# A decoder block on one core: a third pair of k tiles by seven products in the gate/up blocks, moves issued by Pool, own places for those weights, and PSUM banks that alternate

## The chip, the cores and the metric

The kernel runs on one core of a Trainium2 chip. Its time is the device time of one execution in microseconds (us). The kernel before took 1382.08 us, the median of three runs (1381.11 to 1382.55).

## The reference, cut to what matters

One decoder layer on 256 rows of width 2048: two attention mixers, a gated sum of them, LayerNorm, then a SwiGLU sublayer and a second LayerNorm. The change lies in the first half of the SwiGLU sublayer, whose hidden width is 5632 (11 blocks of 512 columns):

```
def _swiglu(h, w_ffn_in, w_ffn_out):
    g, u = jnp.split(h @ w_ffn_in, 2, axis=-1)
    return (jax.nn.silu(g) * u) @ w_ffn_out

h = _layer_norm(DEEPNORM_ALPHA * h + _swiglu(h, w_ffn_in[l], w_ffn_out[l]), ln2_g[l], ln2_b[l])
```

All is float32.

## The kernel before, in words

**Products.** A float32 product is made of three matmuls in the type fp32r. Each operand is split into a rounded part and the rest: `split` casts on ScalarE (L71) and subtracts on VectorE (L72). `mm3` (L91 to L93) adds high x high, high x low and low x high into one bank. The 256 rows are two row tiles m of 128, the depth of 2048 is sixteen k tiles of 128. The rows stand still in TensorE; weights stream through, 512 columns a matmul.

**The gate/up blocks.** Block j (0 to 10) makes the 512 gate columns and the 512 up columns of its number for both row tiles, so four sums: c11, c12 (gate and up of row tile 0), c21, c22 (row tile 1). Block 0 is made in another way. For j = 1 to 10 `pair_product` goes over eight pairs of k tiles. For each it loads four tiles of 128 x 512 in one DMA of 1 MB (`load_pair`, L697): gate and up columns of the two k tiles. A plain pair has two splits of 1024 columns, g and u, and eight `mm3`, which are 24 matmuls.

**A pair by seven.** The four sums over one pair are a 2 x 2 by 2 x 2 product of blocks, and seven products of sums of blocks can stand in for eight. The pairs named in `SEVEN` do this in blocks 1 to 9. VectorE builds four sums of weight tiles in place in the loaded tile (L737 to L740, a chain in which each step needs the one before), then these are split too (names t2 and t3): 128 x 1024 twice. So such a pair has three splits of 1024, one of 512 (u: only one of the two up tiles is needed as it is) and the chain of four, and seven `mm3`, which are 21 matmuls. The sums of rows that they need are made and split once, in `row_forms`. Four of the seven products don't belong to one sum alone: they gather over all pairs by seven of the block in four banks of their own (`ps_`, products 1, 6, 7 and 5). After the last pair by seven of a block L751 to L755 join these into four tiles p1, u2, u3 and u4, and at the block's end L758 to L761 add them to the banks c11 to c22. A sigmoid (L774) and two multiplications per row tile follow (L775, L787), then a transpose of 32 x 32 blocks into the tile rt (L264), of which there is one (tag tab). Sixteen DMAs (`move_blocks`, L286) carry rt into act, the input of the output product. `later(8, ...)` places them in the program eight ticks on; a plain pair and a pair by seven tick twice each.

**Buffers.** Weights as loaded: three places (tag raw). Split weights: eight for the high part and eight for the low part (tags wh, wl), each 128 x 1024. Scratch of 128 x 512: eight (tag s). PSUM: four banks of tag acc (c11 to c22) and four of tag tmp (the products). Tag big: twelve places of 8 KB a partition, which in the gate/up blocks hold hres (2), hth and htl (the normalised rows, high and low, 4), the row forms (1), and act, one tile for two blocks.

**Order.** The order on each engine in these blocks is set by a planner, not by hand. It takes instructions in the order of the program, and lets later ones go first where an earlier one isn't ready in its own estimate. SP issues all DMAs of these blocks: loads of weights and moves. After block 10 the output product follows (names fo, oacc): 44 k tiles, the first row tile in acc, the second in tmp from the third k tile on; its rows (ahl, tag s) are split from act.

The functions that the diff touches and what calls them:

Of the kernel before, what the change touches and what calls it, by code (L numbers as in the profile page):

```python
# [11 lines left out]
F32 = mybir.dt.float32  # L12
F32R = mybir.dt.float32r
# [4 lines left out]
P = 128  # L18
# [11 lines left out]
N = 512  # L30
# [14 lines left out]
def decoder_block(ctx, tc, xT, x, wz, lam_qk, subln, wa, wb, wo, g1, b1, b1T, wf, wfp, wfo, g2, b2,  # L45
                  cs_a, cs_b, out):
    nc = tc.nc
    const = ctx.enter_context(tc.tile_pool(name="const", bufs=1))
    wp = ctx.enter_context(tc.tile_pool(name="wp", bufs=8))
    big = ctx.enter_context(tc.tile_pool(name="big", bufs=12))  # L50
    sp = ctx.enter_context(tc.tile_pool(name="sp", bufs=8))
# [3 lines left out]
    def bigt(shape, dt, name):  # L55
        return big.tile([P] + shape, dt, tag="big", name=name)

    def scr(name):
        return sp.tile([P, N], F32, tag="s", name=name)
# [4 lines left out]
    def acc(name):  # L64
        return ps.tile([P, N], F32, tag="acc", name=name)

    def tmp(name):
        return ps.tile([P, N], F32, tag="tmp", name=name)

    def split(src, hi, lo, eng=None):  # L70
        nc.scalar.copy(hi, src)  # L71
        (eng or nc.vector).tensor_sub(lo, src, hi)  # L72
# [17 lines left out]
    def mm3(ac, xh, xl, wh, wl, start, stop):  # L90
        nc.tensor.matmul(ac, xh, wh, start=start, stop=False)  # L91
        nc.tensor.matmul(ac, xh, wl, start=False, stop=False)  # L92
        nc.tensor.matmul(ac, xl, wh, start=False, stop=stop)  # L93
# [10 lines left out]
    def tick():  # L104
        clock[0] += 1
        if queue and queue[0][0] <= clock[0]:
            queue.pop(0)[1]()
# [175 lines left out]
    def move_blocks(dst, rt):  # L283
        for i in range(4):
            for b in range(4):
                nc.sync.dma_start(dst[32 * b:32 * b + 32, i], rt[32 * i:32 * i + 32, b])  # L286

    def qk_block(blk, cs, half, qk, w, name):
        first = blk == 0
# [363 lines left out]
    def stat_h(m, kt):  # L653
        return hth[m][:, kt, :], htl[m][:, kt, :]
# [15 lines left out]

    SEVEN = (2, 4)
    forms = []

    def row_forms():
        ns = len(SEVEN)
        full = bigt([NM, 2 * ns, P], F32, "hfull")
        fs = bigt([4, ns, P], F32, "forms")
        hl = bigt([2, 4, ns, P], F32R, "formshl")  # L680
        for m in range(NM):
            for n, i in enumerate(SEVEN):
                nc.vector.tensor_add(full[:, m, 2 * n:2 * n + 2, :], hth[m][:, 2 * i:2 * i + 2, :], htl[m][:, 2 * i:2 * i + 2, :])
        a = [[full[:, m].rearrange("p (n t) q -> p n t q", t=2)[:, :, t, :] for t in range(2)] for m in range(NM)]
        nc.vector.tensor_add(fs[:, 0], a[1][0], a[1][1])
        nc.vector.tensor_sub(fs[:, 1], fs[:, 0], a[0][0])
        nc.vector.tensor_sub(fs[:, 2], a[0][0], a[1][0])
        nc.vector.tensor_sub(fs[:, 3], a[0][1], fs[:, 1])
        split(fs, hl[:, 0], hl[:, 1])
        forms.append(hl)  # L690

    def stat_s(f, n):
        return forms[0][:, 0, f - 1, n, :], forms[0][:, 1, f - 1, n, :]

    def load_pair(j, i):
        raw = wp.tile([P, 4, N], F32, tag="raw", name="raw_fp%d_%d" % (j, i), bufs=3)
        nc.sync.dma_start(raw.rearrange("p a n -> p (a n)"), wfp[j - 1][i])  # L697
        return raw

    def halves(src, name):  # L700
        n = src.shape[1]
        wh = wp.tile([P, 2, N], F32R, tag="wh", name="wh" + name)
        wl = wp.tile([P, 2, N], F32R, tag="wl", name="wl" + name)
        split(src, wh[:, 0:n], wl[:, 0:n])
        return [(wh[:, a, :], wl[:, a, :]) for a in range(n)]


    def pair_product(j):
        nk = KD // 2
        seven = SEVEN if j < NB_F - 1 else ()  # L710
        c11, c12, c21, c22 = [acc("acc_f%s_%d" % (c, j)) for c in ("g0", "u0", "g1", "u1")]
        ps_ = {}
        for i in range(nk):
            nm = "fp%d_%d" % (j, i)
            raw = load_pair(j, i)
            k0, k1 = 2 * i, 2 * i + 1
            first, final = i == 0, i == nk - 1
            if i not in seven:
                b11, b21 = halves(raw[:, 0:2], nm + "g")
                b22, b12 = halves(raw[:, 2:4], nm + "u")  # L720
                for ac, m, w0, w1 in ((c11, 0, b11, b21), (c12, 0, b12, b22), (c21, 1, b11, b21), (c22, 1, b12, b22)):
                    mm3(ac, *stat_h(m, k0), *w0, first, False)
                    mm3(ac, *stat_h(m, k1), *w1, False, final)
                tick()
                tick()
                continue
            n = seven.index(i)
            s0, s1 = n == 0, n == len(seven) - 1
            if s0:
                for f in (1, 6, 7, 5):  # L730
                    ps_[f] = tmp("p%d_%d" % (f, j))
            b11, b21 = halves(raw[:, 0:2], nm + "g")
            b22, = halves(raw[:, 2:3], nm + "u")
            mm3(ps_[1], *stat_h(0, k0), *b11, s0, s1)
            mm3(c11, *stat_h(0, k1), *b21, False, False)
            mm3(c12, *stat_s(4, n), *b22, False, False)
            nc.vector.tensor_sub(raw[:, 2], raw[:, 2], raw[:, 3])  # L737
            nc.vector.tensor_sub(raw[:, 3], raw[:, 3], raw[:, 0])
            nc.vector.tensor_add(raw[:, 0], raw[:, 2], raw[:, 0])
            nc.vector.tensor_sub(raw[:, 1], raw[:, 1], raw[:, 0])  # L740
            t2, t4 = halves(raw[:, 0:2], nm + "t2")
            t3, t1 = halves(raw[:, 2:4], nm + "t3")
            tick()
            mm3(ps_[6], *stat_s(2, n), *t2, s0, s1)
            mm3(ps_[7], *stat_s(3, n), *t3, s0, s1)
            mm3(ps_[5], *stat_s(1, n), *t1, s0, s1)
            mm3(c21, *stat_h(1, k1), *t4, False, False)
            tick()
            if s1:
                p1, u2, u3, t = [scr("%s_%d" % (c, j)) for c in ("p1", "u2", "u3", "u4")]  # L750
                nc.scalar.copy(p1, ps_[1])  # L751
                nc.vector.tensor_add(u3, p1, ps_[6])
                nc.vector.tensor_add(u2, u3, ps_[7])
                nc.vector.tensor_add(u3, u3, ps_[5])
                nc.vector.tensor_add(t, u2, ps_[5])  # L755
        if not seven:
            return (c11, c12), (c21, c22)
        nc.vector.tensor_add(p1, p1, c11)  # L758
        nc.vector.tensor_add(u3, u3, c12)
        nc.vector.tensor_add(u2, u2, c21)  # L760
        nc.vector.tensor_add(t, t, c22)  # L761
        return (p1, u3), (u2, t)

    act = []
    for j in range(NB_F):
        if j % 2 == 0:

            act.append(bigt([2, 4, NM, 4, 32], F32, "act%d" % (j // 2)))
        rt = None
        ts_ = []  # L770

        def silu(m, gate):
            t = scr("sl%d_%d" % (j, m))
            nc.scalar.activation(t, gate, AF.Sigmoid)  # L774
            nc.vector.tensor_mul(t, t, gate)  # L775
            return t
        if j == 0:
            ts_ = [silu(m, ga[m]) for m in range(NM)]
            later(3, row_forms)
            ups = product(wf[1], KD, stat_h, "fu0")  # L780
        else:
            rows = pair_product(j)
            ts_ = [silu(m, rows[m][0]) for m in range(NM)]
            ups = [rows[m][1] for m in range(NM)]
        rt = sp.tile([P, 4, NM, P], F32, tag="tab", name="rt%d" % j, bufs=1)
        for m in range(NM):
            nc.vector.tensor_mul(ts_[m], ts_[m], ups[m])  # L787
            turn_blocks(rt, m, ts_[m])
        later(8, lambda j=j, rt=rt: move_blocks(act[j // 2][:, j % 2].rearrange("p i m h c -> p i (m h c)"),
                                                rt.rearrange("p b m n -> p b (m n)")))  # L790
# [97 lines left out]
    with tc.manual_schedule():  # L888
# [26 lines left out]
        j = NB_D - 1  # L915
# [74 lines left out]
```

## Time and profile before

| | us |
|---|---|
| median of three runs | 1382.08 |
| profiled execution | 1384.11 |
| its span, first to last instruction | 1382.3 |
| TensorE busy (PE) | 1365.0 |
| VectorE busy (DVE) | 916.9 |
| ScalarE busy (ACT) | 644.5 |
| GpSimd busy (POOL) | 57.2 |

The mean granted clock of TensorE is 0.998. The gate/up blocks 1 to 10 lie between 705 and 1132 us of the span. Times in rows count from the span's start. A matmul's row shows 0.39 us, but the next may start before it has ended; so what counts is the distance from start to start. The same holds on VectorE for instructions that don't wait for each other.

### The profile page before, as it was taken

Reading aid. Unit: us, or ns where it says so; the run is one execution under the profiler, and the core shown is the slowest. Engines: PE = TensorE matmul, PEld = TensorE weight load, DVE = VectorE, ACT = ScalarE, POOL = GpSimd, SP = SyncE. Lnnn points to the kernel's source line nnn. Section 1 sums busy time; section 2 is a strip of 40 time slices with the busy share of each in tenths; the row PEclk is TensorE's granted clock in tenths of the full one; section 3 lists DMA queues with packets and bytes.
Section 4 is the critical chain, followed back from the end, with each engine's and each line's share of the span. In section 5 each row is a group of like instructions: output and inputs, shape, how many; then the busy total and the mean of one; then the engine's idle time right before and its main releaser. Section 6 shows DMA issues by size and latency. Waiting matters only on the chain.

```text
span 1382.3 us, 16276 instructions
## 1 busy us (share of the span) xinstructions
PE 1365.0 (99%) x6110; PEld 1126.0 (81%) x6110; DVE 916.9 (66%) x1161; ACT 644.5 (47%) x866; POOL 57.2 (4%) x64
## 2 busy tenths in 40 slices
PE   8999999999999999999999999999999999999997
PEld 6888888888888888888888888888788788888886
DVE  6666566766645454575878888888787765554555
ACT  4463444546444434443644455445454444444441
POOL 0001010100000000100000000000000000000003
PEclk9999999999999999999999999999999999999999
DMA  8583645464454649663445664546745676555541
GB/s 281 192 302 145 223 166 198 179 217 152 156 225 162 249 138 356 221 244 122 161 161 192 248 244 182 195 171 247 254 170 195 230 280 225 206 186 191 205 152 61
DMA packets 57151, 279.45 MB, mean 202 GB/s; under 512 B 10224, under 2 KB 22640, under 8 KB 25712
## 3 DMA queue, kind: packets, MB, share of 16 engines
q1 hardware_dynamic: 56784, 278.08, 55.2%
q8 instruction: 48, 0.79, 0.2%
q10 hardware_dynamic: 288, 0.33, 0.1%
q14 instruction: 31, 0.25, 0.1%
HBM read 264.74 MB, written 2.10 MB: 193 GB/s over the span
## 4 chain that ended last, share of the span: by engine, by line
PE 79%; DVE 9%; DMA 7%; ACT 2%; issue 2%; SPq 1%; POOL 0%; POOLq 0%; ACTq 0%; DVEq 0%
PE oacc L91 6%; PE oacc L93 6%; PE oacc L92 6%; DMA raw_fp<-in_wfp 5%; PE acc_fu L91 3%; PE acc_fu L93 3%; PE acc_fu L92 3%; PE acc_fg L91 3%; PE acc_fg L93 3%; PE acc_fg L92 3%; PE acc_gA L91 2%; PE acc_gB L93 2%; PE acc_gA L93 2%; PE acc_gA L92 2%; PE acc_gB L92 2%; PE acc_gB L91 2%
## 5 line engine op out<-in xcount | busy, mean ns | idle before, releaser
L72 DVE TENSOR_TENSOR wl_fo<-raw_fo,wh_fo 128x1024 fp32r<-128x1024 f32 x84 | 102.5, 1225 | 98.5 <-ACT wh_fo L71 93.4
L71 ACT CAST wh_fo<-raw_fo 128x1024 fp32r<-128x1024 f32 x84 | 88.2, 1055 | 115.4 <-PE oacc L93 99.2
L93 PE MATMUL oacc<-wh_fo,ahl 128*128 128x512 f32 x332 | 129.3, 389 | 0.0
L91 PE MATMUL oacc<-wh_fo,ahl 128*128 128x512 f32 x332 | 129.2, 389 | 0.0
L92 PE MATMUL oacc<-wl_fo,ahl 128*128 128x512 f32 x332 | 129.2, 389 | 0.0
L93 PEld LDWEIGHTS oacc<-wh_fo,ahl 128*128 128x128 f32 x332 | 62.3, 188 | 13.4 <-DVE ahl L72 0.3
L91 PEld LDWEIGHTS oacc<-wh_fo,ahl 128*128 128x128 f32 x332 | 62.3, 188 | 12.9
L92 PEld LDWEIGHTS oacc<-wl_fo,ahl 128*128 128x128 f32 x332 | 62.3, 188 | 12.9
L72 DVE TENSOR_TENSOR wl_gA<-raw_gA,wh_gA 128x1024 fp32r<-128x1024 f32 x32 | 38.9, 1220 | 35.9 <-ACT wh_gA L71 35.7
L72 DVE TENSOR_TENSOR wl_o<-raw_o,wh_o 128x1024 fp32r<-128x1024 f32 x32 | 39.5, 1235 | 33.9 <-ACT wh_o L71 33.9
L71 ACT CAST wh_gA<-raw_gA 128x1024 fp32r<-128x1024 f32 x32 | 33.6, 1054 | 53.3 <-PE acc_brB L93 20.0
L71 ACT CAST wh_o<-raw_o 128x1024 fp32r<-128x1024 f32 x32 | 33.7, 1054 | 48.5 <-PE acc_o L93 33.9
L72 DVE TENSOR_TENSOR wl_gB<-raw_gB,wh_gB 128x1024 fp32r<-128x1024 f32 x32 | 38.6, 1222 | 19.9 <-ACT wh_gB L71 19.3
L91 PE MATMUL acc_o<-wh_o,mth 128*128 128x512 f32 x128 | 50.4, 394 | 0.0
L91 PE MATMUL acc_gA<-wh_gA,xth 128*128 128x512 f32 x128 | 50.2, 392 | 0.0
L91 PE MATMUL acc_gB<-wh_gB,xth 128*128 128x512 f32 x128 | 50.1, 391 | 0.0
L93 PE MATMUL acc_o<-wh_o,mtl 128*128 128x512 f32 x128 | 49.9, 390 | 0.0
L92 PE MATMUL acc_o<-wl_o,mth 128*128 128x512 f32 x128 | 49.8, 389 | 0.0
L93 PE MATMUL acc_gB<-wh_gB,xtl 128*128 128x512 f32 x128 | 49.8, 389 | 0.0
L92 PE MATMUL acc_gA<-wl_gA,xth 128*128 128x512 f32 x128 | 49.8, 389 | 0.0
L92 PE MATMUL acc_gB<-wl_gB,xth 128*128 128x512 f32 x128 | 49.8, 389 | 0.0
L93 PE MATMUL acc_gA<-wh_gA,xtl 128*128 128x512 f32 x128 | 49.8, 389 | 0.0
(515 smaller groups left out, 3761.9 us busy)
## 6 DMA issues: line engine op xcount, KB each, us to landing
raw_fp<-in_wfp SPq DMA_DIRECT2D x80, 1024.0 KB, 5.9
raw_fo<-in_wfo SPq DMA_DIRECT2D x44, 1024.0 KB, 4.8
raw_gA<-in_wz SPq DMA_DIRECT2D x16, 1024.0 KB, 4.9
raw_gB<-in_wz SPq DMA_DIRECT2D x16, 1024.0 KB, 5.0
raw_o<-in_wo SPq DMA_DIRECT2D x16, 1024.0 KB, 4.8
raw_vA<-in_wz SPq DMA_DIRECT2D x8, 1024.0 KB, 5.1
raw_qB<-in_wz SPq DMA_DIRECT2D x8, 1024.0 KB, 6.9
raw_kB<-in_wz SPq DMA_DIRECT2D x8, 1024.0 KB, 5.2
```

What stands on the lines that cost most here:

```text
L71: nc.scalar.copy(hi, src)
L72: (eng or nc.vector).tensor_sub(lo, src, hi)
L91: nc.tensor.matmul(ac, xh, wh, start=start, stop=False)
L92: nc.tensor.matmul(ac, xh, wl, start=False, stop=False)
L93: nc.tensor.matmul(ac, xl, wh, start=False, stop=stop)
```

## The change

`SEVEN` names three pairs, 2, 4 and 6 (the third, fifth and seventh). The row forms have a third set, in two tiles of tag s. The moves of a block go out from GpSimd's queue. In blocks 1 to 7 the loaded weights of a pair by seven have a place of tag big instead of one of the three of tag raw. In odd blocks the sums lie in the banks of tag acc and the products in those of tag tmp, in even blocks the other way round.

```
     def move_blocks(dst, rt):
         for i in range(4):
             for b in range(4):
-                nc.sync.dma_start(dst[32 * b:32 * b + 32, i], rt[32 * i:32 * i + 32, b])
+                nc.gpsimd.dma_start(dst[32 * b:32 * b + 32, i], rt[32 * i:32 * i + 32, b])
...
-    SEVEN = (2, 4)
+    SEVEN = (2, 4, 6)
...
-        hl = bigt([2, 4, ns, P], F32R, "formshl")
+        hl = bigt([2, 4, 2, P], F32R, "formshl")
+        more = [[sp.tile([P, 4, P], F32R, tag="s", name="forms%d_%d" % (n, k)) for k in range(2)] for n in range(2, ns)]
...
-        split(fs, hl[:, 0], hl[:, 1])
-        forms.append(hl)
+        split(fs[:, :, 0:2], hl[:, 0], hl[:, 1])
+        for n in range(2):
+            forms.append([hl[:, k, :, n] for k in range(2)])
+        for n, hi_lo in enumerate(more):
+            split(fs[:, :, 2 + n], *hi_lo)
+            forms.append(hi_lo)
...
     def load_pair(j, i):
-        raw = wp.tile([P, 4, N], F32, tag="raw", name="raw_fp%d_%d" % (j, i), bufs=3)
+
+        if i in SEVEN and j < 8:
+            raw = bigt([4, N], F32, "raw_fp%d_%d" % (j, i))
+        else:
+            raw = wp.tile([P, 4, N], F32, tag="raw", name="raw_fp%d_%d" % (j, i), bufs=3)
...
-        c11, c12, c21, c22 = [acc("acc_f%s_%d" % (c, j)) for c in ("g0", "u0", "g1", "u1")]
+
+        acc_c, acc_p = (acc, tmp) if j % 2 else (tmp, acc)
+        c11, c12, c21, c22 = [acc_c("acc_f%s_%d" % (c, j)) for c in ("g0", "u0", "g1", "u1")]
...
-                    ps_[f] = tmp("p%d_%d" % (f, j))
+                    ps_[f] = acc_p("p%d_%d" % (f, j))
```

## Rows read from the trace of the kernel before

**Rows 1.** The page, parts 1 and 2: busy time of engines; TensorE's granted clock.

```profile
PE 1365.0 (99%) x6110; PEld 1126.0 (81%) x6110; DVE 916.9 (66%) x1161; ACT 644.5 (47%) x866; POOL 57.2 (4%) x64
...
PEclk9999999999999999999999999999999999999999
```

**Rows 2.** Timeline of TensorE, block 1: start, duration, line, output and inputs.

```profile
710.70 0.39 PE L91 MATMUL acc_fg<-whfp_1g,hth 128*128 128x512 f32 x1
...
715.91 0.39 PE L93 MATMUL acc_fu<-whfp_1u,htl 128*128 128x512 f32 x1
716.14 0.39 PE L91 MATMUL p<-whfp_2g,hth 128*128 128x512 f32 x1
...
720.90 0.39 PE L91 MATMUL acc_fg<-whfp_3g,hth 128*128 128x512 f32 x1
```

**Rows 3.** Busy time by stretch: PE, PEld, DVE, ACT, POOL; block 3.

```profile
789.00:831.00 42.00, 42.00 (x187) 34.79 (x186) 35.83 (x43) 20.91 (x23) 0.00 (x0) 1.00 0.58 212
```

**Rows 4.** Timeline of VectorE, block 7, pairs 3 and 4; in brackets: idle before.

```profile
968.26 1.22 DVE L72 TENSOR_TENSOR wlfp_3g<-raw_fp,whfp_3g 128x1024 fp32r<-128x1024 f32 x1
...
970.53 1.22 DVE L72 TENSOR_TENSOR wlfp_4g<-raw_fp,whfp_4g 128x1024 fp32r<-128x1024 f32 x1
...
972.39 0.69 DVE L737 TENSOR_TENSOR raw_fp<-raw_fp 128x512 f32<-128x512 f32 x1
...
974.57 0.69 DVE L740 TENSOR_TENSOR raw_fp<-raw_fp 128x512 f32<-128x512 f32 x1
976.46 2.36 DVE L72 TENSOR_TENSOR wlfp_4t<-raw_fp,whfp_4t 128x1024 fp32r<-128x1024 f32 x2 [1.20 <-ACT whfp_4t L71]
```

**Rows 5.** Timeline of VectorE, the end of block 7.

```profile
985.69 0.68 DVE L752 TENSOR_TENSOR u<-p,p 128x512 f32<-128x512 f32 x1
986.47 0.69 DVE L753 TENSOR_TENSOR u<-u,p 128x512 f32<-128x512 f32 x1
...
1001.07 0.68 DVE L758 TENSOR_TENSOR p<-p,acc_fg 128x512 f32<-128x512 f32 x1
1001.66 0.68 DVE L737 TENSOR_TENSOR raw_fp<-raw_fp 128x512 f32<-128x512 f32 x1
...
1006.47 0.70 DVE L264 STREAM_TRANSPOSE rt<-sl 128x512 f32<-128x512 f32 x1
1007.10 0.65 DVE L787 TENSOR_TENSOR sl<-sl,u 128x512 f32<-128x512 f32 x1
```

**Rows 6.** Timeline of ScalarE, the end of block 10 and the output product's start.

```profile
1126.98 1.06 ACT L71 CAST wh_fo<-raw_fo 128x1024 fp32r<-128x1024 f32 x1 [0.31 <-PE acc_fu L93]
...
1131.06 0.60 ACT L774 ACTIVATE sl<-acc_fg 128x512 f32<-128x512 f32 x1 [2.12 <-PE acc_fg L93]
1131.55 1.01 ACT L71 CAST ahl<-act 128x256 fp32r<-128x256 f32 x3
```

**Rows 7.** Views of the tiles act and ln2g: issues, ns, first and last start.

```profile
L286 SPq DMA_DIRECT2D act<-rt x176: 507/589/1592, 709.7 to 1144.2; - x176
...
L795 SPq DMA_DIRECT2D ln2g<-in_g x1: 382/382/382, 1074.2 to 1074.2; - x1
```

**Rows 8.** Timeline of VectorE and TensorE, block 1, pair 4.

```profile
722.04 2.36 DVE L72 TENSOR_TENSOR wlfp_4t<-raw_fp,whfp_4t 128x1024 fp32r<-128x1024 f32 x2 [1.20 <-ACT whfp_4t L71]
...
729.06 0.39 PE L91 MATMUL p<-whfp_4t,formshl 128*128 128x512 f32 x1
```

**Rows 9.** Waits of TensorE, whole span: total, times, longest.

```profile
PE acc_fg L91 <- DVE p L758: 2.4, 3, 1.4
```

**Rows 10.** Waits of SP's queue, 747 to 1088 us.

```profile
SPq L286 <- DVE rt L264: 89.1, 8, 11.9
```

**Rows 11.** Timeline of SP's queue, block 4.

```profile
836.37 10.95 SPq L286 DMA_DIRECT2D act<-rt  x16
847.42 16.30 SPq L697 DMA_DIRECT2D raw_fp<-in_wfp  x6
```

**Rows 12.** View of the tile raw_fp: its loads.

```profile
DMA to landing us min/median/max: 4.7/5.9/7.7
```

More of the change, by code (lines that the diff above doesn't have):

```diff
@@ L688, in row_forms @@
         nc.vector.tensor_sub(fs[:, 3], a[0][1], fs[:, 1])
-        split(fs, hl[:, 0], hl[:, 1])
-        forms.append(hl)
+        split(fs[:, :, 0:2], hl[:, 0], hl[:, 1])
[4 more added lines that the diff above has]
+            forms.append(hi_lo)
     def stat_s(f, n):
-        return forms[0][:, 0, f - 1, n, :], forms[0][:, 1, f - 1, n, :]
+        return tuple(t[:, f - 1, :] for t in forms[n])
     def load_pair(j, i):
-        raw = wp.tile([P, 4, N], F32, tag="raw", name="raw_fp%d_%d" % (j, i), bufs=3)
+        if i in SEVEN and j < 8:
+            raw = bigt([4, N], F32, "raw_fp%d_%d" % (j, i))
+        else:
+            raw = wp.tile([P, 4, N], F32, tag="raw", name="raw_fp%d_%d" % (j, i), bufs=3)
         nc.sync.dma_start(raw.rearrange("p a n -> p (a n)"), wfp[j - 1][i])
```

## The prediction

> **What bounds the kernel now.** I read the page first: TensorE is busy 1365.0 of 1382.3 us at the full granted clock, VectorE 916.9 [rows 1]. So a matmul less is time less, as long as nobody else becomes late. I then read the gate/up blocks, the only stretch that the diff touches, from the timeline of TensorE: a pair of k tiles done plainly takes 5.44 us (710.70 to 716.14), one done by seven products 4.76 us (716.14 to 720.90) [rows 2]. A block j = 1 to 9 is now six plain pairs and two by seven: 6 x 5.44 + 2 x 4.76 = 42.16 us, and TensorE fills it. The table by block shows the engine behind it: in a 42 us stretch VectorE is busy 35.83 us where all its records are there (43), and ScalarE 20.91 [rows 3]. VectorE is thus the engine to watch, and its timeline prices a pair. A plain pair is two splits, 968.26 to 970.53: 2.27 us. A pair by seven starts at 970.53 and its last split starts 1.14 after 976.46 and leaves VectorE 1.14 later, at 978.74: 8.21 us, of which 1.20 is idle, waiting for ScalarE's cast of what VectorE itself has just written [rows 4]. The end of a block is fourteen more instructions (L752 to L755, L758 to L761, two each of L775, L787 and the transpose), 0.59 to 0.78 us from start to start: 8.6 us [rows 5].
>
> Before: 6 x 2.27 + 2 x 8.21 + 8.6 = 38.6 us of VectorE per block, 2.4 of it the two waits, so 36.2 of work. That is 0.2 to 0.4 over the 35.83 of the table, as the chain runs tighter where other instructions stand between its steps; I take 0.3 off below. It fits into 42.16 with 3.9 us to spare.
>
> **The change, part by part.**
>
> *The third pair by seven.* TensorE: 5.44 - 4.76 = 0.68 us per block, nine blocks: 6.1 us less. A block then asks 41.48 us of TensorE. VectorE: 5 x 2.27 + 3 x 8.21 + 8.6 = 44.6, less 0.3: 44.3 us. So the bound changes sides: VectorE is 2.8 us short in each block, 9 x 2.8 = 25.2 us. The bounds: if all three waits of 1.20 us are filled with other work, VectorE asks 44.3 - 3.6 = 40.7 and nothing is short (0); if nothing else changes it is 9 x (44.6 - 41.48) = 28.1. I take 25.2, since the waits are there in the rows and I see nothing that may fill them. What could is the split of the next pair, whose cast ScalarE could do while VectorE works at the chain. But the trace shows that a tile gets its place only after the earlier tiles of the same tag have been begun: the casts of act (tile ahl), whose first data were moved from 709.7 us on, start at 1131.55 in a row of three, right behind the second sigmoid of the last block at 1131.06, which writes the tile named before them, while casts of weights that come later in the program ran before it [rows 6, 7]. In the same way the load of ln2g, which needs nothing but a place, comes only at 1074.2 [rows 7]. By that order the cast of pair 5 can't pass the casts of pair 4's sums, and the waits stay.
>
> Against the shortage stands VectorE's lead at the start: in j = 1 the last split of pair 4 ends at 722.04 + 2.36 = 724.40, and TensorE first takes that tile at 729.06, 4.7 us later [rows 8]. The longer row forms (two adds of 256, four wider by 128, a split of 512: as much as three instructions of 512, 3 x 0.6 = 1.8 us) eat part of it. I take 3.5 us, bounds 2.9 and 4.7.
>
> *Banks that change sides.* Now the sums of a block go into the banks that the block before has just left, and TensorE waits where VectorE is late to read them: 2.4 us, three times, for L758 [rows 9]. The list leaves out 0.16 us of each: the next matmul could start 0.23 us after the last, whose mark is 0.39 us long [rows 2]; so the three cost 2.4 + 3 x 0.16 = 2.9 us. With the swap the next block begins in the banks of the products, read out a pair earlier: 2.9 us less, bounds 0 and 2.9. What is late next is the split itself.
>
> *Moves by Pool.* SP now waits for rt (89.1 us in eight blocks) [rows 10] and then spends 10.95 us on sixteen issues before the next load of weights goes out at 847.42 [rows 11]. Without them the loads of pairs 5 and 6 leave about 10 us earlier, and VectorE loses its waits for weights. That is worth nothing on TensorE's side now, and I have not counted those waits above, so it adds nothing; without it the shortage would be larger by up to 2 us a block. Pool has no work in these blocks (0.00 us [rows 3]). No row shows a move issued by Pool. From SP's 0.59 us an issue [rows 7], sixteen take at least 9.5 us; they must be done before the next block's transposes want rt, some 41 us later, so up to 2.5 us each costs nothing. I take nothing.
>
> *Own raw places.* The twelve places of the tag big hold, in these blocks, hres (2), hth and htl (4), the forms (1) and one act per two blocks, which takes its place when the moves of its even block go out, early in the odd block. That leaves three for the weights up to j = 4, two in j = 5 and 6, and one in j = 7. With two, pair 6 takes the place that pair 2 left long ago: nothing. With one, pair 4's load in j = 7 starts when pair 2's last split is done, and VectorE has only pair 3 (2.27 us) until it wants it. A load takes 5.9 us (4.7 to 7.7) to land [rows 12], the cast 1.06 [rows 6] and a hand-over about 0.1: 5.9 + 1.16 - 2.27 = 4.8 us idle, and the same for pair 6: 9.6 us, bounds 0 (the lead hides it) and 13. VectorE being the bound, I take 9.6.
>
> Sum: 1384.1 - 6.1 + 25.2 - 3.5 - 2.9 + 9.6 = 1406.4 us for a profiled execution; that of before lies 2.0 over the median of the timed runs (1382.08), so 1404 us.
>
> **The rivals.** *A: the waits are filled* (faster). If ScalarE casts the next plain pair during the chain, VectorE has 1.14 us of work for each 1.20 us of waiting and asks 40.7 us of a block. It decides from 2.8 of the 3.6 us filled. For it: weights of pairs 5 and 7 are there early now, and in a block where TensorE takes every tile at once there are free tiles for casts. Against it: rows 6 and 7. Then 6.1 and 2.9 us go and up to 4 stay where three pairs of 8.21 follow each other: 1373 to 1378. *B: as A, but one place in j = 7*: the two waits of 4.8 us stay, little lead against them: 1381 to 1387. *C: the waits stay, but the weights of j = 7 are there in time* (a place that I have counted as taken is free): 1404 - 9.6, about 1394. *D: Pool is slow at issuing.* Over 2.5 us a move, rt holds up the transposes and with them VectorE, by 16 us per block for each us over it: past 1412. Against it: Pool is empty there, and a transpose of 512 with one input (0.63 from L264's start to the next) goes no faster than an add with two [rows 5], so no instruction of VectorE in these blocks runs in a faster mode that might keep others out. The Trainium skill (SBUF — State Buffer, section SBUF: two separate sides) warns of moves issued from GpSimd: its cores write the descriptors and are locked out while VectorE runs an instruction in a mode with both ports. By that rule these rows leave Pool free, and the sum stays; no run so far shows it.
>
> **Chances.** Forecast 0.46, A 0.22, B 0.12 (half of it within the bound of no change), C 0.16, D 0.04. A difference under 0.2% (2.8 us) can't be told from none. Faster: A, 0.22. Same: half of B, 0.06. Slower: the rest, 0.72. The forecast's own range is 1397 to 1412 (28.1 for 25.2 and 13 for 9.6 above; more lead below). For 8 in 10 it has to take in C and B and the upper edge of A: 1377 to 1412.
>
> **What would show it.** Right: in blocks j = 3 to 9 VectorE idle mostly at 1.2 us before the splits of the sums, three per block; TensorE waiting for VectorE's splits (L92 after L72), most at the start of a block behind the fourteen end instructions and in j = 7; blocks of 44 us instead of 41.5, j = 7 near 52. Casts of pair 5 standing in ScalarE's order before those of pair 4's sums would show A. No wait of TensorE for L758 to L761 shows the swap right. L286 on Pool, with SP's loads in a steady row, shows the moves right; transposes waiting for act's moves show D. My forecast is wrong if TensorE's stretch from 705 us to the first matmul of the output product is shorter than now.

## The result and the profile after

The changed kernel takes 1414.3 us (median; 1413.22 to 1414.8), the kernel before 1382.3: ratio 1.0227, 95% interval 1.0208 to 1.0245. Slower, as forecast, but 10 us over the 1404.0 and 2.3 over the range. The profiled execution took 1413.83 us, 29.7 more than that of before (1384.11).

The page of the changed kernel, parts 1 and 2, against [rows 1]:

```profile
PE 1373.1 (97%) x6083; PEld 1127.2 (80%) x6083; DVE 960.8 (68%) x1218; ACT 653.4 (46%) x885; POOL 143.6 (10%) x240
...
PE   9999999999999999999999989998799899999996
...
PEclk9999999999999999999999999999999999999998
```

TensorE has 27 matmuls less, yet is busy 8 us longer: matmuls became slower somewhere. A digit of the clock's line is a mean over 35 us and hides it. VectorE works 43.9 us more. Waits of TensorE from 700 to 1165 us (who waits for whom: us in total, times, longest), against the one row of [rows 9]:

```profile
PE acc_fg L92 <- DVE wlfp_0g L72: 15.3, 4, 4.7
PE p L91 <- ACT whfp_6t L71: 3.1, 2, 2.9
PE acc_fu L92 <- DVE wlfp_0u L72: 1.7, 1, 1.7
PE p L91 <- ACT whfp_2g L71: 1.3, 1, 1.3
...
```

The wait for L758 (now L769; lines shift by 11) is gone; in its place TensorE stands at the start of blocks 4, 7, 8 and 10 before the first split of weights. Timelines of VectorE and TensorE at the start of block 4 (start, duration; in brackets: idle before):

```profile
831.00 1.29 DVE L798 TENSOR_TENSOR sl<-sl,u 128x512 f32<-128x512 f32 x2
832.20 1.30 DVE L264 STREAM_TRANSPOSE rt<-sl 128x512 f32<-128x512 f32 x2
833.42 1.18 DVE L72 TENSOR_TENSOR wlfp_0g<-raw_fp,whfp_0g 128x1024 fp32r<-128x1024 f32 x1
```

```profile
829.59 0.39 PE L91 MATMUL acc_fg<-whfp_0g,hth 128*128 128x512 f32 x1
...
830.50 0.39 PE L91 MATMUL p<-whfp_2g,hth 128*128 128x512 f32 x1
834.66 0.80 PE L92 MATMUL acc_fg<-wlfp_0g,hth 128*128 128x512 f32 x1 [3.77 <-DVE wlfp_0g L72]
...
835.68 0.63 PE L91 MATMUL acc_fg<-whfp_0g,hth 128*128 128x512 f32 x1
836.11 0.63 PE L92 MATMUL acc_fg<-wlfp_0g,hth 128*128 128x512 f32 x1
...
840.29 0.39 PE L92 MATMUL acc_fg<-wlfp_0g,hth 128*128 128x512 f32 x1
840.51 0.39 PE L93 MATMUL acc_fg<-whfp_0g,htl 128*128 128x512 f32 x1
```

The split stands behind the end of block 3, as forecast. What the forecast did not have is what comes after the wait: the matmuls follow each other at 0.43 us instead of 0.23. Busy time by stretch there (PE, PEld, DVE, ACT, POOL; then the granted clock):

```profile
826.00:830.00 4.00, 4.00 (x19) 3.23 (x18) 4.00 (x8) 4.00 (x6) 0.00 (x0) 1.00 0.91 301
...
835.00:840.00 5.00, 5.00 (x13) 3.84 (x13) 4.96 (x6) 0.00 (x0) 4.65 (x10) 0.50 0.75 213
840.00:845.00 5.00, 5.00 (x23) 4.16 (x22) 3.70 (x6) 2.23 (x3) 1.97 (x4) 0.98 0.89 307
```

The granted clock is 0.50 there, the level of 1.2 GHz; it falls like that five times in the blocks, each time during or behind a pause of 3.1 to 4.8 us (a pause is the distance from one matmul's start to the next, less the 0.23 us of the full clock). Summing what all distances between matmul starts in the blocks have over 0.23 us, 26.7 us are pauses and 11.6 are matmuls at the slow clock. The books of the 29.7: -6.1 matmuls, -4.0 waits of before, +26.7 pauses, +11.6 slow clock, +1.9 at the end (below), -0.4 other. The lateness isn't spread evenly, as the forecast's 44 us a block would have it: from start to start blocks 4 to 9 take 48.1, 41.6, 44.0, 48.7, 53.5 and 42.8 us.

VectorE's waits before the splits of the sums are there as claimed from [rows 4], by line over blocks 2 to 9 (busy, mean ns, then idle before; 9.5 for 6t):

```profile
L72 DVE TENSOR_TENSOR wlfp_2t<-raw_fp,whfp_2t 128x1024 fp32r<-128x1024 f32 x16 | 18.9, 1222 | 9.6 <-ACT whfp_2t L71 9.6
L72 DVE TENSOR_TENSOR wlfp_4t<-raw_fp,whfp_4t 128x1024 fp32r<-128x1024 f32 x16 | 18.9, 1221 | 9.6 <-ACT whfp_4t L71 9.6
```

### The profile page after: what moved, and what is told of

It is laid out like the page before. It is cut to its first block, busy times and chain, and to the rows that moved or that the text cites. A ratio compares the mean times of both kernels' runs of the same rounds, so it can differ in the third digit from the quotient of the medians.

```text
span 1411.6 us, 16368 instructions
## 1 busy us (share of the span) xinstructions
PE 1373.1 (97%) x6083; PEld 1127.2 (80%) x6083; DVE 960.8 (68%) x1218; ACT 653.4 (46%) x885; POOL 143.6 (10%) x240
## 4 chain that ended last, share of the span: by engine, by line
PE 45%; DVE 5%; issue 1%; ACT 1%; DMA 0%; POOL 0%; DVEq 0%; POOLq 0%; ACTq 0%
PE oacc L93 6%; PE oacc L91 6%; PE oacc L92 6%; PE acc_fg L92 4%; PE acc_fg L93 4%; PE acc_fg L91 4%; PE acc_fu L92 4%; PE acc_fu L93 4%; PE acc_fu L91 4%; PE p L92 2%; PE p L93 1%; PE p L91 1%; DVE sl L786 0%; DVE rt L264 0%; DMA raw_fp<-in_wfp 0%
## 5 line engine op out<-in xcount | busy, mean ns | idle before, releaser
L286 POOL DMA_DIRECT2D act<-rt x176 | 86.3, 498 | 422.2 <-DVE rt L264 246.0
L71 ACT CAST whfp_2t<-raw_fp 128x1024 fp32r<-128x1024 f32 x18 | 18.0, 1049 | 90.2 <-DVE raw_fp L751 76.5
```

The source lines that it names most:

```text
L286: nc.gpsimd.dma_start(dst[32 * b:32 * b + 32, i], rt[32 * i:32 * i + 32, b])
```

## The experiments

Unless said otherwise each is an edit of the changed kernel. The kernel before was timed anew beside them: 1380.2 us beside e1 to e4, 1380.9 beside e5 to e8, 1381.5 beside e9 to e12, 1381.1 beside e13 and e14. Ratios are to these; differences between kernels of two such groups, or to the changed kernel (1382.3), carry an uncertainty of up to some 2 us.

**e1, two pairs by seven.**

```diff
-    SEVEN = (2, 4, 6)
+    SEVEN = (2, 4)
```

> The changed kernel with SEVEN = (2, 4): two pairs by seven again; moves by Pool, own raw places for pairs 2 and 4 up to j = 7 and the swap stay. Theory (the third seven pair made VectorE the bound; its pauses also halve the granted clock): the waits and the drops of the clock in the gate/up blocks go. 1384.1 profiled in the kernel before, less 3.9 us of waits for L758 that the swap removes, plus 1.9 us for the longer end of Pool: 1380 to 1384 us. Rival P (moves by Pool slow VectorE or hold up the transposes): 1395 us or more with two seven pairs too. Rival Q (the own raw places are the main cause): j = 7 still shows pauses of TensorE of some 4 us before pairs 4, 1388 to 1395 us.

1382.0 us, ratio to before 1.0013 (1.0004 to 1.0022). No wait of TensorE is left in the blocks, and no slow clock. Pool's moves don't slow VectorE: it is busy 917.8 us, against 916.9 [rows 1]. The blocks take 4.0 us less than before, by TensorE's starts, but 1.9 of it come back at the end: from the first matmul of the output product on it takes 252.0 us instead of 250.1. Why it is not 2 us faster all the same stays open; in the profiled run the first matmul of block 1 already comes later than before, at 706.67 us instead of 705.26.

**e2, no own raw places.**

```diff
-        if i in SEVEN and j < 8:
+        if i in SEVEN and j < 0:
```

> The changed kernel without the own raw places: all raw weights of the pairs in the three places of tag raw. Theory: only the pauses of j = 7 (and what follows them in j = 8) change: 8 to 10 us less, 1404 to 1407 us, drops of the granted clock in the other blocks stay. Rival Q (the own places are the main cause): 1390 us or less. Rival R (the own places give loads an early start, and without them VectorE waits for weights in every block): 1420 us or more.

1409.7 us, 4.6 less than the changed kernel: less than the 8 to 10 expected. The pauses are now in blocks 4, 6, 8 and 10, with the slow clock behind each.

**e3, moves by SyncE** (`nc.sync` again in `move_blocks`).

> The changed kernel with the moves of act issued by SyncE again. Theory of the prediction: with VectorE as the bound each late load counts, so the 10 us in which SyncE issues sixteen moves cost up to 2 us in each of nine blocks: 1415 to 1435 us; the end, which Pool's last drain now sets 1.9 us later, comes back by that. Rival P (Pool's issues beside VectorE cost time): faster than the changed kernel by 5 us or more, 1409 us or less.

1430.0 us, ratio 1.036 (1.0344 to 1.0375): 15.7 more, within the theory. P falls.

**e4, no swap** (`acc_c, acc_p = acc, tmp`).

> The changed kernel with the sums always in banks acc and the products in tmp. Theory: the four last adds of a block free the banks that the next block begins in, but the split of its first weights stands behind the same adds in VectorE's order, so TensorE waits about as long as with the swap: 1413 to 1418 us. Rival S (with VectorE late the swap is worth more than before): TensorE waits for L769 to L772 at each block's start and loses 2 to 4 us more per block, 1425 us or more.

1413.7 us, not to be told from the changed kernel; no wait for L769 to L772. With VectorE late, the swap is worth nothing.

**e5, the next pair between chain and sums** (on e2; cut to the lines that load and split it).

```diff
...
+            r2 = load_pair(j, i + 1)
+            n2 = "fp%d_%d" % (j, i + 1)
+            nxt = r2, (halves(r2[:, 0:2], n2 + "g"), halves(r2[:, 2:4], n2 + "u"))
             t2, t4 = halves(raw[:, 0:2], nm + "t2")
...
```

> e2 (no own raw places) with one change of order: inside a pair by seven the next plain pair is loaded and split between the four subtractions and the splits of the sums, so that VectorE has 2.3 us of work where it waited 1.2 us. Theory (in e2 VectorE is the bound from block 3 on, with 45.6 us a block where TensorE asks 41.48; 3.6 of it are the three waits): VectorE asks about 42 us, TensorE's pauses and the drops of its clock all but vanish: 1376 to 1385 us, against 1409.7 in e2. Rival W (VectorE's order is bound by something else, such as late weights): less than 10 us gained, 1400 us or more.

1393.3 us: 16.4 gained, 8 short of the theory. The edit gave the work, but not its place. Timeline of VectorE in block 5 and its waits over blocks 2 to 9:

```profile
893.02 1.22 DVE L72 TENSOR_TENSOR wlfp_5g<-raw_fp,whfp_5g 128x1024 fp32r<-128x1024 f32 x1
894.16 0.69 DVE L749 TENSOR_TENSOR raw_fp<-raw_fp 128x512 f32<-128x512 f32 x1
894.76 1.22 DVE L72 TENSOR_TENSOR wlfp_5u<-raw_fp,whfp_5u 128x1024 fp32r<-128x1024 f32 x1
...
897.34 0.69 DVE L752 TENSOR_TENSOR raw_fp<-raw_fp 128x512 f32<-128x512 f32 x1
899.23 1.22 DVE L72 TENSOR_TENSOR wlfp_4t<-raw_fp,whfp_4t 128x1024 fp32r<-128x1024 f32 x1 [1.19 <-ACT whfp_4t L71]
```

```profile
DVE wlfp_6t L72 <- ACT whfp_6t L71: 7.3, 6, 1.4
```

The planner put the next pair's splits among the subtractions, where nothing was waiting, and the wait at the end stayed, in six blocks of eight (for 4t and 2t too: 7.2 us in six waits each). Two pauses of TensorE are followed by the slow clock here, the first of them in block 7 (timeline, then the stretch behind it):

```profile
963.91 0.39 PE L91 MATMUL p<-whfp_2g,hth 128*128 128x512 f32 x1
966.62 0.80 PE L92 MATMUL acc_fu<-wlfp_0u,hth 128*128 128x512 f32 x1 [2.32 <-DVE wlfp_0u L72]
...
966.60:969.80 3.20, 3.18 (x8) 2.51 (x9) 3.20 (x3) 0.00 (x0) 3.20 (x7) 0.50 0.67 202
```

That pause is 2.5 us from start to start less 0.23, shorter than any that brought the slow clock in the changed kernel.

**e6, the kernel before with the swap alone.**

> The kernel before with the swap of the banks alone. Theory: the three waits for L758 to L761 (3.9 us with what lies between the marks) go and nothing else changes: 1376.0 to 1377.0 us where the kernel before takes 1380.2 (0.28% less). Rival: the same adds hold up the next split, and TensorE waits for that: no difference within 0.1%.

1379.2 us, ratio 0.9987 (0.9978 to 0.9996): faster, by half of what was expected. The interval reaches into the rival's 0.1%, but the rival's reason falls: in its trace no wait is left, and the blocks take 422.97 us instead of 426.97. The profiled run of before (1384.11) lies above its median; that its other runs had shorter waits is a guess.

**e7, two products on Pool** (on e2).

```diff
-            nc.vector.tensor_mul(ts_[m], ts_[m], ups[m])
+            (nc.gpsimd if 0 < j < NB_F - 1 else nc.vector).tensor_mul(ts_[m], ts_[m], ups[m])
```

> e2 with the two multiplications of a block that take gate times up (L798 twice, 0.6 us each on VectorE) done by Pool in blocks 1 to 9. Theory (VectorE is the bound, and the slow clock of TensorE costs nothing while VectorE is late anyway): 9 x 1.2 = 10.8 us less than e2, 1397 to 1401 us. Rival H (pauses and the halved clock after them add up, and shorter pauses spare the clock too): 1395 us or less. Rival N (VectorE isn't the bound at the block's end): 1407 us or more.

1407.5 us, 2.2 under e2 instead of 10.8. Rival N's number, but not its reason. By line, blocks 2 to 9, first e2, then e7 (mean ns is the last number before the second bar):

```profile
L72 DVE TENSOR_TENSOR wlfp_0g<-raw_fp,whfp_0g 128x1024 fp32r<-128x1024 f32 x7 | 8.4, 1202 | 0.0
L786 DVE TENSOR_TENSOR sl<-sl,u 128x512 f32<-128x512 f32 x7 | 4.8, 688 | 1.8 <-ACT sl L785 1.6
```

```profile
L72 DVE TENSOR_TENSOR wlfp_0g<-raw_fp,whfp_0g 128x1024 fp32r<-128x1024 f32 x7 | 11.1, 1583 | 0.0
L786 DVE TENSOR_TENSOR sl<-sl,u 128x512 f32<-128x512 f32 x8 | 9.4, 1169 | 0.1
...
L798 POOL TENSOR_TENSOR sl<-sl,u 128x512 f32<-128x512 f32 x16 | 23.4, 1467 | 245.3 <-DVE sl L786 245.3
```

VectorE's instructions beside Pool's multiplications became longer: 0.38 and 0.48 us here, and 0.20, 0.10 and 0.08 for wlfp_0u, wlfp_1u and wlfp_2g, together 1.24 us a block where 1.2 was taken off. The Trainium skill (SBUF — State Buffer, section SBUF: two separate sides) names a port pair shared by VectorE and GpSimd, held for a whole instruction, among others by a VectorE operation with two inputs in SBUF against a GpSimd operation that reads SBUF. These rows agree; that Pool's moves took nothing (in the changed kernel 25 of the 104 steps of the chain, L748 to L751, lie beside a move, and both they and the others take 0.69 us) agrees too.

**e8, pauses of several sizes** (on e1 without own places).

```diff
+    MORE = {2: 6, 4: 8, 6: 10, 8: 12}
...
             nc.vector.tensor_sub(raw[:, 2], raw[:, 2], raw[:, 3])
+            for _ in range(MORE.get(j, 0) // 2 if i == 4 else 0):
+                nc.vector.tensor_add(raw[:, 2], raw[:, 2], raw[:, 3])
+                nc.vector.tensor_sub(raw[:, 2], raw[:, 2], raw[:, 3])
```

> e1 (two pairs by seven, TensorE without a pause) without own places, and with 6, 8, 10 and 12 more adds and subtractions (0.72 us each) in the chain of pair 4 in blocks 2, 4, 6 and 8: they take as much away as they add. The sums of pair 4 have a lead of 4.2 us, so TensorE should pause about 0.1, 1.6, 3.0 and 4.4 us. Theory: a pause of 1.6 us leaves the granted clock at full, those of 3.0 and 4.4 us are followed by some 3 to 7 us at half of it, which TensorE, being the bound here, loses on top: 9 us of pauses and 3 to 7 us of slow clock, 1393 to 1398 us. Rival: the clock has another cause than the pause, and the price is the pauses alone, 1390 to 1392 us.

1391.5 us in one run, which as a number is the rival's (1390 to 1392), because the pauses came out at 0, 0.5, 2.2 and 4.0 us, up to 1.1 under the plan. The trace decides: 7.2 us of pauses and 2.8 of slow clock over the blocks of e1, where 9 and 3 to 7 were expected. Stretches around the third pause (two of 1.8 and 0.4 us with matmuls between them) and the fourth:

```profile
938.90:942.30 3.40, 1.53 (x6) 0.65 (x5) 2.20 (x4) 2.44 (x3) 0.00 (x0) 1.00 0.00 0
942.30:950.00 7.70, 7.70 (x36) 6.28 (x35) 7.70 (x9) 5.19 (x6) 0.00 (x0) 1.00 0.67 224
...
1026.00:1029.90 3.90, 0.09 (x2) 0.01 (x1) 2.63 (x5) 1.10 (x2) 0.00 (x0) 0.85 0.00 0
1029.90:1035.60 5.70, 5.70 (x13) 4.29 (x14) 4.67 (x5) 4.68 (x5) 0.00 (x0) 0.50 0.38 137
```

The clock stays at 1.00 through and behind the pause in block 6; in block 8 it falls within the longer pause and is 0.50 behind it. Nothing in the program but the length of VectorE's chain differs between these blocks, so the longer pause brings the slow clock, and where TensorE is the bound both are paid.

**e9, the sums split early.** The second subtraction has already written what products 7 and 5 need.

```diff
             nc.vector.tensor_sub(raw[:, 3], raw[:, 3], raw[:, 0])
+            t3, t1 = halves(raw[:, 2:4], nm + "t3")
             nc.vector.tensor_add(raw[:, 0], raw[:, 2], raw[:, 0])
             nc.vector.tensor_sub(raw[:, 1], raw[:, 1], raw[:, 0])
             t2, t4 = halves(raw[:, 0:2], nm + "t2")
-            t3, t1 = halves(raw[:, 2:4], nm + "t3")
             tick()
-            mm3(ps_[6], *stat_s(2, n), *t2, s0, s1)
             mm3(ps_[7], *stat_s(3, n), *t3, s0, s1)
             mm3(ps_[5], *stat_s(1, n), *t1, s0, s1)
+            mm3(ps_[6], *stat_s(2, n), *t2, s0, s1)
```

> The changed kernel (own raw places and all) with one edit: in a pair by seven the sums for products 7 and 5 are split as soon as the second of the four subtractions has written them, and TensorE takes products 7 and 5 ahead of 6. ScalarE then casts them beside the third and fourth subtraction, and VectorE has no wait of 1.20 us. Theory (VectorE is the bound; these 3 x 1.2 us a block are the shortage): VectorE asks 45.6 - 3.6 = 42.0 us a block against 41.48, and its lead of 13 us at block 2 covers 9 x 0.5; left are the two waits for raw places in block 7: 1376 to 1383 us, against 1414.3. Rival H (the halved clock is caused by something else and stays): 1385 us or more. Rival W (another bound takes over): 1395 us or more.

1386.1 us, 28 under the changed kernel, 3 over the theory's range and just inside rival H's. But H's reason falls: all pauses but those of block 7 and the start of 8 are gone, and with them the slow clock, which is left in one place, behind the pause of 3.2 us at block 8. VectorE's waits in block 7:

```profile
DVE wlfp_4g L72 <- ACT whfp_4g L71: 4.4, 1, 4.4
DVE wlfp_6g L72 <- ACT whfp_6g L71: 3.8, 1, 3.8
```

**e10, e9 without own places.**

> e9 without own raw places. Theory: no pause of TensorE in the gate/up blocks: e1 without its pauses at 1382.0, less 9 x 0.68 = 6.1: 1375 to 1378 us, 0.2 to 0.4% under the kernel before. Rival: without the places VectorE waits for weights (blocks 4 to 8), 1380 us or more.

1374.8 us, ratio 0.9954 (0.994 to 0.9968): faster than both kernels. TensorE waits for nothing in the blocks, which take 416.85 us: 6.1 less than in e6. A pair by seven on VectorE, against [rows 4]:

```profile
800.88 1.22 DVE L72 TENSOR_TENSOR wlfp_4g<-raw_fp,whfp_4g 128x1024 fp32r<-128x1024 f32 x1
...
804.18 0.69 DVE L751 TENSOR_TENSOR raw_fp<-raw_fp 128x512 f32<-128x512 f32 x1
804.91 0.69 DVE L752 TENSOR_TENSOR raw_fp<-raw_fp 128x512 f32<-128x512 f32 x1
805.52 2.50 DVE L72 TENSOR_TENSOR wlfp_4t<-raw_fp,whfp_4t 128x1024 fp32r<-128x1024 f32 x2
807.94 1.22 DVE L72 TENSOR_TENSOR wlfp_5g<-raw_fp,whfp_5g 128x1024 fp32r<-128x1024 f32 x1
```

No bracket stands before the split, and the pair takes 7.06 us (800.88 to 807.94) instead of 8.21.

**e11 and e12, e10 with the moves by ScalarE and by SyncE.**

> e10 with the moves of act issued by ScalarE. Theory of the end (Pool's last drain ends 1.9 us later where Pool has issued moves): 1.9 us less than e10, 1373 to 1376 us, if 16 issues of 0.6 us fit into ScalarE's free 20 us of a block. Rival: a burst of 9.5 us of issues holds up casts, VectorE and TensorE wait behind it: 1380 us or more.

> e10 with the moves issued by SyncE. Theory: with VectorE at 42 us of 41.48 the loads that leave 10 us late cost what they cost in e3 against the changed kernel (16 us) less what VectorE's regained 3.6 us a block cover: 1374 to 1385 us. Rival: the late loads cost all of the 16 us here too, 1390 us or more.

1395.5 us, ratio 1.0111 (1.009 to 1.0131), and 1408.0, ratio 1.0185 (1.0164 to 1.0207). Both rivals were right, and on SyncE the late loads cost 33 us, twice the rival's 16. On ScalarE a burst of eleven issues takes 7.58 us, and the cast behind them waits; on SyncE VectorE waits for the weights of pair 4 alone (747 to 1110 us):

```profile
DVE wlfp_4g L72 <- ACT whfp_4g L71: 30.9, 6, 6.4
```

VectorE's digits on e10's page stand at 9 through most of the blocks; that this is why what comes late is not caught up is argued, not shown.

**e13, the pauses filled** (on e2): matmuls that nobody reads stand where TensorE would pause.

```diff
+        for _ in range(16 if j in (4, 6, 8, 10) else 0):
+            nc.tensor.matmul(c22, hth[0][:, 0, :], hth[0][:, 0:4, :].rearrange("p a b -> p (a b)"), start=True, stop=True)
```

> e2 with sixteen more matmuls (0.227 us each, 3.6 us) that nobody reads, ahead of the first pair of blocks 4, 6, 8 and 10, where TensorE paused 4.3 to 4.7 us and its granted clock then fell to half: the pauses shrink to about 1 us and the clock stays at full. Theory (VectorE sets the time, and TensorE's slow stretches lie within its lateness; only the drop in block 10, behind which VectorE is ahead for good, costs its 2.6 us): 1405.5 to 1409 us, against 1409.7 in e2; the pauses of the other blocks grow instead. Rival H (the 9 us of half clock are a cost of their own): 1399 to 1403 us.

1400.4 us, ratio 1.0134 (1.0117 to 1.0151): 9.3 less than e2, with 64 matmuls more. Stretches at the start of block 4, first e2, then e13:

```profile
836.00:842.90 6.90, 6.00 (x14) 4.73 (x15) 6.83 (x8) 0.00 (x0) 5.88 (x12) 0.51 0.59 193
```

```profile
838.00:842.00 4.00, 4.00 (x19) 3.30 (x18) 3.97 (x5) 0.00 (x0) 3.64 (x8) 1.00 0.85 244
```

In e13 the clock stays at 1.00 throughout the blocks, and VectorE, ScalarE, Pool and SyncE's queue do the same work in the same order as in e2, so no other order explains the gain. My theory falls, rival H stands: the slow clock is a cost of its own although VectorE is late. How TensorE's slowness comes back to VectorE shows on ScalarE, block 4, first in e2, then in e13:

```profile
870.82 0.59 ACT L762 COPY p<-p 128x512 f32<-128x512 f32 x1 [1.93 <-PE p L93]
871.31 1.05 ACT L71 CAST whfp_7u<-raw_fp 128x1024 fp32r<-128x1024 f32 x1
```

```profile
868.55 0.57 ACT L764 COPY p<-p 128x512 f32<-128x512 f32 x1
869.02 1.05 ACT L71 CAST whfp_7u<-raw_fp 128x1024 fp32r<-128x1024 f32 x1
```

In e2 the copy of product 1 waits for the slow TensorE, the cast of pair 7 stands behind the copy, and VectorE waits 1.87 us for that cast; in e13 none of this happens. These waits for 7u come to 3.6 us in three blocks; in block 10 the slow matmuls cost TensorE itself 2.7. How the rest of the 9.3 comes about was not followed up. The Trainium skill (TensorE: Matmul & The Clock Gate, section HAM oscillation — how this bites in real kernels) describes a kernel whose waits for data bring the slow clock back at every tile; e2 agrees, with the slow clock behind its pauses in four blocks, and e13 prices it at 9.3 us.

**e14, e9 with own places up to j = 6** (`j < 7`).

> e9 with own raw places up to j = 6 instead of 7. Theory (of the own places only the single one left in block 7 costs time): as e10, 1374 to 1377 us, against 1386 in e9. Rival: the own places cost in other blocks too, 1380 us or more.

1374.7 us, ratio 0.995 (0.9935 to 0.9965): as e10. So the single place in block 7 is the whole cost of the own places, 11.3 us in e9 (against e10).

## Why the prediction was wrong

The kernels form a ladder on which each term of the sum can be laid (e6 1379.2, e10 1374.8, e13 1400.4, e2 1409.7, changed 1414.3):

| step | term of the sum | measured |
|---|---|---|
| swap, before to e6 | -2.9 | -1.7; 0 in the changed kernel (e4) |
| third pair on TensorE and the moves, VectorE's waits closed, e6 to e10 | -6.1 | -4.4: -6.1 in the blocks, +1.9 at the end |
| VectorE's three waits open, e10 to e13 | +25.2 - 3.5 = 21.7 | +25.6 |
| slow clock behind the pauses, e13 to e2 | none | +9.3 |
| own places, e2 to changed | +9.6 | +4.6 |

The steps cross groups of runs (above). By the lengths of the blocks in the traces (426.97, 422.97, 416.85, 442.38, 451.78 and 455.11 us) they are -4.0, -6.1, +25.5, +9.4 and +3.3.

**The step that failed is the sum itself:** "6.1 + 25.2 - 3.5 - 2.9 + 9.6" counts TensorE's waits as if TensorE came out of each at full speed. It has no term for the granted clock, which [rows 1] shows at full throughout, because the kernel before hardly ever paused in these blocks (2.4 us in all, [rows 9]). The change brought pauses of over 3 us, and they brought the slow clock: 9.3 us in e13's comparison, 11.6 by the gaps in the changed kernel's own trace. That this is about the size of the miss, 10 us, is in part luck: the other four terms are off by +1.2, +1.7, +3.9 and -5.0 us, which nearly cancel.

**VectorE** as the new bound was right, and the waits stay open as forecast. The reason given, that the casts of the next pair can't pass those of the sums as long as they come later in the program, fits e5, where they come earlier and do; no run tests the rule of places by itself. Where the clock stays up, in e13, blocks 4 to 9 take (1101.84 - 833.99) / 6 = 44.6 us: the sum as it stood before 0.3 us was taken off to make it 44.3. With the slow clock it is 45.6 in e2 and, own places included, 46.5 in the changed kernel. The waits' whole cost, 25.6, is 3.9 over the term: the 0.3 us a block is 2.7 of that in nine blocks, and of 9 x (44.6 - 41.48) = 28.1 it leaves 2.5 us for VectorE's lead, for which 3.5 was taken; no run measures the lead by itself.

**The moves by Pool** were costed at nothing, against up to 2 us a block without them. e3 shows 15.7, as bounded. The miss is small and elsewhere: Pool's last drain (DRAIN, a record of its queue at the kernel's end). Its rows by line, the changed kernel and then the one before (ns min/median/max, first and last start):

```profile
L997 POOLq DRAIN  x3: 34/102/5476, 1405.4 to 1411.3; - x3
```

```profile
L986 POOLq DRAIN  x3: 39/78/961, 1378.0 to 1382.1; - x3
```

Where Pool has issued moves the longest drain takes 5.5 us (5.47 in e10, 0.97 in e3, whose moves are SyncE's), and the end comes 1.9 us later. Every kernel with Pool's moves here shows this loss, e1 and e10 included: from the first matmul of the output product on it takes 252.0 to 252.3 us, without Pool's moves 249.9 to 250.1.

**The own places**: the mechanism was right and in block 7 alone (e14), with waits of 4.4 and 3.8 us in e9, 3.8 and 3.7 in the changed kernel, where I gave 4.8. The step that failed is adding them in full to the shortage: they cost 11.3 us in e9, where nothing else is late, and 4.6 in the changed kernel, in which e2 pauses at block 8 anyway; that the two overlap is argued, not shown.

**The swap** did what it says: the three waits of [rows 9], with the smaller gaps beside them 4.0 us by the starts of matmuls, are gone. In the sum it was over-rated, as it pays only while TensorE is the bound.

**The rivals**: A's time (1373 to 1378) is that of e10, but it took an edit to fill the waits; I had looked for other work to put there and not seen that the chain's own second half will do. D did not occur: a move on Pool takes 0.50 us.

## What to carry to other kernels

When a change makes an off-path engine the bound, price the tensor engine's pauses twice: once as waits, once as the slow matmuls behind the longer ones, and add what comes back through its readers. Before giving a chain of dependent steps more work to hide behind, look whether a part of its results is ready earlier: splitting two of the four sums two steps sooner turned, with the own places left out as well, a loss of 2.3% into a gain of 0.5%. When you move an elementwise operation to Pool, look at the durations of VectorE's instructions beside it: in e7 they grew by what was taken off.

## What the runs showed of the hardware

Pauses of TensorE of 1.8 us (changed kernel) and of 2.2 in two parts (e8) left the granted clock at 1.00; one of 2.5 us (e5) and those of 3.1 to 4.8 us (changed kernel) went with a fall to 0.50, at which matmuls follow each other at 0.43 us instead of 0.23. In e2, block 4, two pauses of 2.0 and 2.8 us with one matmul between them did the same. Sixteen matmuls that nobody reads at each of four pauses were worth 9.3 us (e13). Two multiplications of 128x512 on Pool, 1.47 us each, lengthened VectorE's instructions beside them by 1.24 us a block, as much as they took off it (e7). A kernel whose Pool issued transfers ends 1.9 us later (252.0 against 250.1 us for the same output product).
